# Two encoder layers on one core: the MLP up projection's and the norms' subtractions on VectorE alone, and the second half of the output projection's operands loaded after its first weights

## The chip, the cores and the metric

The kernel runs on one core of a Trainium2 chip. A core has TensorE (PE in the profile, its weight loads PEld), VectorE (DVE), ScalarE (ACT), GpSimd (POOL) and SyncE (SP), whose queue issues the DMAs here. The engines run side by side, each through its own instructions in order, and wait for one another by semaphores. The metric is the device time of one execution in microseconds (us), the median of several runs; lower is better.

## The reference

The trunk has two layers on a sequence of 1024 tokens with 1024 features, in float32. Layer 0 mixes tokens by softmax attention, layer 1 by a gated DeltaNet in both directions; behind each mixer comes a gated MLP with a three-tap convolution:

```python
for i in range(DEPTH):
    y = rmsnorm(h, norm_mix[i])
    h = h + (attention_mixer(y, ...) if i % 2 == 0 else gated_deltanet_mixer(y, ...))
    h = h + conv_ffn(rmsnorm(h, norm_ffn[i]), ...)
return rmsnorm(h, norm_final)

def conv_ffn(h, w_up, conv_w, conv_b, w_down):
    u = depthwise_conv_centred(h @ w_up, conv_w, conv_b)
    a, b = jnp.split(u, 2, axis=-1)
    return (jax.nn.silu(a) * b) @ w_down
```

The DeltaNet ends with `o.reshape(B, S, GDN_V_W) @ w_out`, a projection from 16 heads of 128 to 1024 features.

## The kernel before

**Splits.** A matmul in full precision is made of three in a reduced float32 format. `split` (lines 108 to 110) makes of an operand a rounded part hi (a cast on ScalarE, line 109) and a rest lo = operand - hi (a subtraction on the engine that is passed in, line 110); `dense` (line 134) multiplies hi by hi, hi by lo and lo by hi. Every weight tile and every operand is split so while the kernel runs. In the profile the weights' parts are wh and wl, the tokens' yh and yl, or base (hi) and a lo beside it.

**MLP.** The up projection (`UpProjection`) multiplies 2 x 2 blocks with seven products in place of eight: p1 to p7 with sums and differences of the blocks as operands. `tokens` makes the token side once per layer: the norm's multiplication (line 190), differences of halves (`sub`, line 899), and the splits (`put`) into operands 11, 21, t1, t2, t3, t4 and 22 (t4 and 22 lie in tiles named base). `run` goes over 22 pairs of column tiles f. For each, `operands` loads four weight blocks (a) and makes four sums (s, line 978), `product` splits a sum and issues twelve matmuls into a PSUM bank, and the banks are drained into ua and ub (`first_sum`, line 960, and line 998 on VectorE, copies on ScalarE). Then the convolution (lines 1029 and 1031), the gate's product (line 1035), and `DownProjection.take`, which stores tiles of the result and, in every second f, four differences of them (line 1057) to DRAM. The down projection loads these back as its operands (raw<-g, line 1084). The work of consecutive f overlaps.

In this version GpSimd has a part of those subtractions: in `tokens` every third one, in `operands` the first and third sum, in `product` the splits of p6 and p4, in `take` all four, and in `norm` (line 212) the split of every second tile.

**Output projection of the DeltaNet.** At the end of `gdn` the heads' outputs od lie in DRAM. The first eight heads are multiplied while the last heads are still computed, with partial sums stored as x. For the last eight, `split_rows` loads each od row and splits it, first the first half of the tokens for all eight, then the second half, through three staging tiles t. Then `out_proj` goes over three token ranges (`PARTS`: 512, 256 and 256 tokens) and eight output tiles m: weights (line 121), 24 matmuls, residual from x (line 343), addition (line 344), squares for the next norm. The last partial sums of the first eight heads are added on VectorE (line 818) and stored (line 819) just before.

**Order.** A scheduler sorts all instructions of an engine by priorities, mostly the order of the code; `ahead` raises it. SP issues all loads and stores in one queue in order, so a store that waits for its data holds every load behind it. Tiles of a pool turn round: a load into a staging tile waits until its former content was read.

## Time and profile before

| | |
|---|---|
| median of 3 runs | 3449.74 us (3447.62 to 3450.36) |
| the profiled execution | 3439.26 us, its span 3437.5 us |
| TensorE busy | 3247.3 us, 94% of the span |
| VectorE busy | 2495.2 us, 73% |
| ScalarE busy | 1741.5 us, 51% |
| GpSimd busy | 842.4 us, 25% |

The up projections lie at about 640 to 1090 and 2745 to 3205 us, the DeltaNet from 1310 to 2630, its last output projection from 2644 to 2745. Of a row of the timeline the first number is the start in us from the span's start and the second the duration of the group, with a count behind x where several alike are merged; in brackets stands how long the engine was idle before it, and the instruction that ended that. A matmul's duration is longer than its distance to the next one, since matmuls are pipelined.

### The profile page before, as it was taken

To read this page: it belongs to the slowest core of one execution; us is meant where nothing else is said; L and a number is where in the kernel's file an instruction comes from. 1 tells how busy PE (TensorE), PEld (TensorE's weight loads), DVE (VectorE), ACT (ScalarE), POOL (GpSimd) and SP (SyncE) were. 2 spreads that over 40 slices of the span, in tenths; PEclk is the share of its full clock that TensorE was granted. 3 is DMA by queue.
4 is the path that set the end of the run, shared out by engine and by line. 5 is a ranking of instruction groups with operands and counts; after the bars stand their busy time and mean duration, and the time that the engine had idled before them with its cause. 6 is when DMAs were issued, how large, how long until landed. Compare 5 with 4: busy or idle time off the path is not lost. (4 is left out here: it accounts for less than half of the span.)

```text
span 3437.5 us, 54135 instructions
## 1 busy us (share of the span) xinstructions
PE 3247.3 (94%) x19690; PEld 2620.0 (76%) x19690; DVE 2495.2 (73%) x4235; ACT 1741.5 (51%) x3224; POOL 842.4 (25%) x919
## 2 busy tenths in 40 slices
PE   7999999899999998899999999999898989999998
PEld 6877788677777876677777777777676867777786
DVE  5335886887776875778778787877853787777695
ACT  4235664544454454565555556666532544544453
POOL 1111330444442002121221212222120144444100
PEclk9999999999999999999999999999999999999999
DMA  3331006333324642332342424334356623332743
GB/s 127 104 113 59 32 31 191 122 106 111 112 94 168 218 129 65 102 111 88 113 126 81 136 92 130 102 113 132 102 175 206 204 98 110 101 105 92 244 132 109
DMA packets 249802, 411.20 MB, mean 120 GB/s; under 512 B 25536, under 2 KB 76096, under 8 KB 249536
## 3 DMA queue, kind: packets, MB, share of 16 engines
q1 hardware_dynamic: 249536, 407.76, 36.6%
q8 instruction: 155, 2.54, 0.3%
q14 instruction: 111, 0.91, 0.1%
HBM read 294.80 MB, written 107.61 MB: 117 GB/s over the span
## 5 line engine op out<-in xcount | busy, mean ns | idle before, releaser
L134 PE MATMUL mm<-base,wh 128*128 128x512 f32 x1248 | 480.1, 412 | 10.0 <-ACT base L109 5.9
L109 ACT CAST wh<-w_raw 128x512 fp32r<-128x512 f32 x275 | 169.9, 619 | 296.7 <-PE mm L134 175.6
L110 DVE TENSOR_TENSOR wl<-w_raw,wh 128x512 fp32r<-128x512 f32 x275 | 193.2, 707 | 138.2 <-ACT wh L109 137.1
L134 PE MATMUL mm<-yh,wh 128*128 128x512 f32 x736 | 282.6, 413 | 5.3 <-ACT t L291 2.7
L134 PE MATMUL mm<-yh,wl 128*128 128x512 f32 x736 | 280.6, 410 | 1.0 <-DVE wl L110 1.0
L134 PE MATMUL mm<-yl,wh 128*128 128x512 f32 x736 | 279.3, 408 | 0.3 <-POOL yl L110 0.2
L134 PEld LDWEIGHTS mm<-base,wh 128*128 128x128 f32 x1248 | 238.3, 191 | 49.6 <-ACT base L109 6.3
L153 POOL TENSOR_TENSOR rs<-rs,power 128x8 f32<-128x8 f32 (+2 forms) x38 | 63.8, 1679 | 824.8 <-DVE rs L152 824.7
L134 PE MATMUL mm<-base,wl 128*128 128x512 f32 x624 | 257.3, 412 | 6.4 <-DVE wl L110 6.4
L703 POOL TENSOR_SCALAR kd<-c,yds 128x128 f32<-128x128 f32 x224 | 95.2, 437 | 635.0 <-PE cp L732 444.8
L109 ACT CAST wh<-a 128x512 fp32r<-128x512 f32 x164 | 101.8, 622 | 256.7 <-PE mm L134 122.6
L109 ACT CAST wh<-s 128x512 fp32r<-128x512 f32 x212 | 131.4, 620 | 183.6 <-PE sp L134 87.3
L134 PE MATMUL sp<-base,wh 128*128 128x512 f32 (+1 forms) x672 | 211.5, 372 | 12.6 <-ACT wh L109 12.6
L448 DVE SCALAR_TENSOR_TENSOR t<-mm,gdn_cw,t 128x1023 f32<-128x1023 f32 (+1 forms) x128 | 163.1, 1276 | 6.8 <-ACT t L445 6.1
L134 PEld LDWEIGHTS mm<-yh,wh 128*128 128x128 f32 x736 | 140.6, 193 | 29.3 <-ACT t L291 3.6
L134 PEld LDWEIGHTS mm<-yl,wh 128*128 128x128 f32 x736 | 140.8, 192 | 27.8 <-POOL yl L110 1.6
L134 PEld LDWEIGHTS mm<-yh,wl 128*128 128x128 f32 x736 | 140.8, 191 | 26.5 <-DVE wl L110 1.7
L134 PE MATMUL sp<-base,wl 128*128 128x512 f32 (+1 forms) x432 | 157.7, 365 | 1.4 <-DVE wl L110 0.9
L134 PEld LDWEIGHTS sp<-base,wh 128*128 128x128 f32 x672 | 127.7, 190 | 34.3 <-ACT wh L109 13.0
L110 DVE TENSOR_TENSOR wl<-s,wh 128x512 fp32r<-128x512 f32 x170 | 142.0, 836 | 12.3 <-ACT wh L109 12.2
L978 POOL TENSOR_TENSOR s<-a,a 128x512 f32<-128x512 f32 x80 | 108.5, 1356 | 159.0 <-DVE s L978 106.0
L134 PEld LDWEIGHTS mm<-base,wl 128*128 128x128 f32 x624 | 119.1, 191 | 27.2 <-DVE wl L110 7.2
(522 smaller groups left out, 9362.4 us busy)
## 6 DMA issues: line engine op xcount, KB each, us to landing
a<-in_ffn_up_dram SPq DMA_DIRECT2D x160, 256.0 KB, 2.8
c<-pk SPq DMA_DIRECT2D x128, 320.0 KB, 3.1
w_raw<-in_gdn_in_dram SPq DMA_DIRECT2D x100, 256.0 KB, 2.8
g_t<-t SPq DMA_DIRECT2D x88, 256.0 KB, 2.0
raw<-g_t SPq DMA_DIRECT2D x88, 256.0 KB, 2.6
w_raw<-in_gdn_out_dram SPq DMA_DIRECT2D x68, 256.0 KB, 3.6
g<-t SPq DMA_DIRECT2D x66, 256.0 KB, 2.1
raw<-g SPq DMA_DIRECT2D x66, 256.0 KB, 2.8
```

The costliest lines, as they stand in the source:

```text
L109: self.nc.scalar.copy(out=hi, in_=src)
L110: (engine or self.nc.vector).tensor_tensor(out=lo, in0=src, in1=hi.bitcast(F32), op=ALU.subtract)
L134: self.nc.tensor.matmul(acc if one else acc[:, hs], lhsT=a, rhs=y[:, hs], start=(first and not onto and k + t == 0), stop=(last and k == n ...
L153: nc.gpsimd.tensor_tensor(out=r, in0=v, in1=self.power[:, :w], op=ALU.pow)
L448: nc.vector.scalar_tensor_tensor(out=o, in0=a, scalar=c[:, i:i + 1], in1=o, op0=ALU.mult, op1=ALU.add)
L703: nc.gpsimd.tensor_scalar(out=kd[:, e], in0=kn, scalar1=col(self.yds, e), scalar2=1.0, op0=ALU.mult, op1=ALU.mult)
L978: e.tensor_tensor(out=s[i], in0=x, in1=z, op=op)
```

## The change

Everything that `norm`, `tokens`, `operands`, `product` and `take` gave to GpSimd is given to VectorE. GpSimd keeps the norms' powers (line 153), the softmax's scaling and the DeltaNet's parts. And `split_rows` is cut in two: of the last eight heads only the first half of the tokens is loaded and split before `out_proj`; the second half is loaded by `rest`, called inside `out_proj` after the first four output tiles, through staging tiles od of its own pool ot.

```diff
@@ norm
-                    self.split(y, ys[k][0][:, hs], ys[k][1][:, hs], nc.gpsimd if k % 2 else nc.vector)
+                    self.split(y, ys[k][0][:, hs], ys[k][1][:, hs], nc.vector)
@@ out_proj
-    def out_proj(self, w, ys, res):
+    def out_proj(self, w, ys, res, rest=None):
...
                                 self.squares(self.h[m][:, cs], cs, m)
+                    if rest and cs.start + m0 == 0:
+                        rest(ot)
@@ gdn
-            os = self.split_rows(self.od[8:], oy, HALVES, lambda: tmp.tile([P, S], F32, name="t")[:, :H2])
+            os = self.halved_rows(oy)
+            self.split_into(os, self.od[8:], HALVES[0], lambda: tmp.tile([P, S], F32, name="t")[:, :H2])
             right.close()
...
-            self.out_proj(lambda m: ap["gdn_out"][m][:, 8:], os, lambda m: x[m])
+            self.out_proj(lambda m: ap["gdn_out"][m][:, 8:], os, lambda m: x[m],
+                          lambda ot: self.split_into(os, self.od[8:], HALVES[1], lambda: ot.tile([P, H2], F32, name="od")))
+    def split_into(self, out, rows, hs, stage):
+        for r, pair in zip(rows, out):
+            t = stage()
+            self.nc.sync.dma_start(out=t, in_=r[:, hs])
+            self.split(t, *(x[:, hs] for x in pair))
@@ tokens
         def sub(x, z, out):
-            engine().tensor_tensor(out=out, in0=x, in1=z, op=ALU.subtract)
+            nc.vector.tensor_tensor(out=out, in0=x, in1=z, op=ALU.subtract)
 
         def put(name, k, xs, x):
             hi, lo = self.b[name][k]
-            t.split(x, hi[:, xs], lo[:, xs], engine())
+            t.split(x, hi[:, xs], lo[:, xs])
@@ operands: the four sums, engines gpsimd, vector, gpsimd, vector
-            e.tensor_tensor(out=s[i], in0=x, in1=z, op=op)
+            nc.vector.tensor_tensor(out=s[i], in0=x, in1=z, op=op)
@@ product
-            self.t.split(x, hi, lo, self.nc.gpsimd if name in ("p6", "p4") else self.nc.vector)
+            self.t.split(x, hi, lo)
@@ take
-        sub = lambda out, x, z: nc.gpsimd.tensor_tensor(out=out, in0=x, in1=z, op=ALU.subtract)
+        sub = lambda out, x, z: nc.vector.tensor_tensor(out=out, in0=x, in1=z, op=ALU.subtract)
```

On SP at the start of the DeltaNet's last output projection, the stores of partial sums (x), the loads of the second half (od) and the first weights (w_raw) stood so:

```order
L831 DMA t<-od_22095 128x512
L819 DMA x_27659<-h 128x512
L831 DMA t<-od_22096 128x512
L831 DMA t<-od_24076 128x512
L831 DMA t<-od_24077 128x512
L831 DMA t<-od_26061 128x512
L819 DMA x_27660<-h 128x512
L831 DMA t<-od_26062 128x512
L831 DMA t<-od_27493 128x512
L831 DMA t<-od_27494 128x512
L121 DMA w_raw<-in_gdn_out_dram 128x512 x5
```

Now the same queue has the following rows. The weights stand right behind the last store, eight of them before the first load of the second half; the other six of its loads follow among later weights.

```order
L819 DMA h<-xd_11460 128x512
L821 DMA x_27659<-h 128x512
L821 DMA x_27660<-h 128x512
L121 DMA w_raw<-in_gdn_out_dram 128x512 x5
L343 DMA res<-x_27653 128x512
L121 DMA w_raw<-in_gdn_out_dram 128x512
L343 DMA res<-x_27654 128x512
L121 DMA w_raw<-in_gdn_out_dram 128x512 x2
L843 DMA od<-od_22095 128x512
L843 DMA od<-od_22096 128x512
```

On VectorE in the up projection, the stretch of one odd f from the first convolution step to the draining of the bank of p1 and p2 (ua<-mm, line 960 before and 965 after) stood so:

```order
L1029 SCALAR_TENSOR_TENSOR t_7578<-ua,ffn_cw,t_7578 128x1023
L1031 SCALAR_TENSOR_TENSOR t_7578<-ua,ffn_cw,t_7578 128x1023
L1029 SCALAR_TENSOR_TENSOR t_7582<-ub,ffn_cw,t_7582 128x1023
L1031 SCALAR_TENSOR_TENSOR t_7582<-ub,ffn_cw,t_7582 128x1023
L110 TENSOR_TENSOR wl<-s,wh 128x512
L1035 TENSOR_TENSOR t_7578<-t_7578,t_7582 128x1024
L978 TENSOR_TENSOR s<-a_7601,s 128x512
L960 TENSOR_TENSOR ua<-mm,ua 128x512
```

Now a split (of p6) stands between the first two steps, and in odd f, as here, one difference of `take` (line 1062) ahead of the draining; an even f has the split alone.

```order
L1034 SCALAR_TENSOR_TENSOR t_7578<-ua,ffn_cw,t_7578 128x1023
L110 TENSOR_TENSOR wl<-s,wh 128x512
L1036 SCALAR_TENSOR_TENSOR t_7578<-ua,ffn_cw,t_7578 128x1023
L1034 SCALAR_TENSOR_TENSOR t_7582<-ub,ffn_cw,t_7582 128x1023
L1036 SCALAR_TENSOR_TENSOR t_7582<-ub,ffn_cw,t_7582 128x1023
L110 TENSOR_TENSOR wl<-s,wh 128x512
L1040 TENSOR_TENSOR t_7578<-t_7578,t_7582 128x1024
L983 TENSOR_TENSOR s<-a_7601,s 128x512
L1062 TENSOR_TENSOR t_7590<-t_7578,t_7428 128x512
L965 TENSOR_TENSOR ua<-mm,ua 128x512
```

## Rows read from the trace of the kernel before

**Rows 1.** Windows: us, busy time of PE, PEld, DVE, ACT, POOL (instructions), clock, DMA
```profile
900.00:950.00 50.00, 49.87 (x214) 39.54 (x213) 38.21 (x39) 26.12 (x37) 23.15 (x15) 1.00 0.33 111
2750.00:2800.00 50.00, 41.68 (x153) 30.61 (x154) 38.38 (x61) 21.84 (x45) 24.49 (x22) 0.90 0.27 88
```

**Rows 2.** Timeline of PE where the DeltaNet's last output projection begins
```profile
2631.51 0.39 PE L134 MATMUL mm<-yh,wl 128*128 128x512 f32 x1
2644.47 1.22 PE L134 MATMUL sp<-base,wh 128*128 128x512 f32 x2 [12.57 <-ACT wh L109]
```

**Rows 3.** Timeline of SP's queue in the same stretch
```profile
2636.70 4.10 SPq L831 DMA_DIRECT2D t<-od  x3
2640.85 3.88 SPq L121 DMA_DIRECT2D w_raw<-in_gdn_out_dram  x5
```

**Rows 4.** Timeline of VectorE and ScalarE in the same stretch
```profile
2629.14 1.35 DVE L110 TENSOR_TENSOR base<-t,base 128x512 fp32r<-128x512 f32 x2 [0.62 <-ACT base L109]
2635.39 0.68 DVE L818 TENSOR_TENSOR h<-mm,h 128x512 f32<-128x512 f32 x1
2643.80 0.62 ACT L109 CAST wh<-w_raw 128x512 fp32r<-128x512 f32 x1
```

**Rows 5.** Windows of the same stretch and just behind it
```profile
2640.00:2650.00 10.00, 5.53 (x15) 4.36 (x16) 4.63 (x8) 4.33 (x7) 0.00 (x0) 0.56 0.80 252
2650.00:2660.00 10.00, 10.00 (x45) 8.27 (x45) 2.74 (x4) 1.87 (x3) 0.00 (x0) 1.00 0.54 188
```

**Rows 6.** Line 978: count, duration ns min/median/max, first and last start
```profile
L978 POOL TENSOR_TENSOR s<-a,a x80: 1282/1292/2273, 672.3 to 3176.5; 128x512 f32<-128x512 f32 x80
L978 DVE TENSOR_TENSOR s<-s,a x40: 693/1688/1782, 673.9 to 3174.0; 128x512 f32<-128x512 f32 x40
L978 DVE TENSOR_TENSOR s<-a,s x40: 678/684/692, 694.0 to 3189.1; 128x512 f32<-128x512 f32 x40
```

**Rows 7.** Timeline of PE, DVE and POOL in one f, and the last f's p5
```profile
901.62 1.74 POOL L110 TENSOR_TENSOR wl<-a,wh 128x512 fp32r<-128x512 f32 x1
903.41 0.50 PE L134 MATMUL sp<-base,wl 128*128 128x512 f32 x1
913.56 0.68 DVE L960 TENSOR_TENSOR ua<-mm,ua 128x512 f32<-128x512 f32 x1
914.00 0.40 PE L134 MATMUL sp<-t23h,wl 128*128 128x512 f32 x1
914.39 0.47 PE L134 MATMUL mm<-t10h,wh 128*128 128x512 f32 x1
...
3190.50 0.47 PE L134 MATMUL mm<-t10h,wh 128*128 128x512 f32 x1
```

**Rows 8.** Timeline of POOL, DVE and PE where both up projections begin
```profile
636.32 0.69 POOL L153 TENSOR_TENSOR rs<-rs,power 128x2 f32<-128x2 f32 x1
656.25 1.43 DVE L110 TENSOR_TENSOR base<-h,base 128x256 fp32r<-128x256 f32 x4
658.49 4.68 DVE L110 TENSOR_TENSOR base<-h,base 128x256 fp32r<-128x256 f32 x4
663.83 0.50 PE L134 MATMUL mm<-base,wl 128*128 128x512 f32 x1 [3.46 <-DVE wl L110]
...
2779.50 0.80 PE L134 MATMUL mm<-base,wl 128*128 128x512 f32 x1 [2.94 <-DVE wl L110]
2812.57 0.71 PE L134 MATMUL mm<-t10h,wh 128*128 128x512 f32 x1 [2.73 <-DVE ua L960]
```

**Rows 9.** Timeline of SP's queue, POOL and PE where both down projections begin
```profile
1093.53 4.53 SPq L1056 DMA_DIRECT2D g_t<-t  x3
1096.42 1.29 POOL L1057 TENSOR_TENSOR t<-t,t 128x512 f32<-128x512 f32 x1 [1.22 <-DMA g<-t]
1105.86 0.67 PE L134 MATMUL mm<-gh,base 128*128 128x512 f32 x1 [2.70 <-ACT base L109]
...
3222.75 0.50 PE L134 MATMUL mm<-gh,base 128*128 128x512 f32 x1 [1.97 <-ACT base L109]
```

More of the change, by code (lines that the diff above doesn't have):

```diff
@@ L808, in gdn @@
                 self.head_out(j, o, dp)
-            os = self.split_rows(self.od[:8], oy, [slice(0, S)], lambda: tmp.tile([P, S], F32, name="t"))
+            os = self.split_rows(self.od[:8], oy, lambda: tmp.tile([P, S], F32, name="t"))
             x = [self.dram.tile([P, S], F32, name=f"x{m}") for m in range(KT)]
@@ L823, in gdn, with split_rows @@
             self.psum = self.banks(sp=4)
-            self.out_proj(lambda m: ap["gdn_out"][m][:, 8:], os, lambda m: x[m])
-    def split_rows(self, rows, pool, parts, stage):
+            self.out_proj(lambda m: ap["gdn_out"][m][:, 8:], os, lambda m: x[m],
+                          lambda ot: self.split_into(os, self.od[8:], HALVES[1], lambda: ot.tile([P, H2], F32, name="od")))
+    def split_rows(self, rows, pool, stage):
         out = self.halved_rows(pool)
-        for ps in parts:
-            for r, pair in zip(rows, out):
-                t = stage()
-                self.nc.sync.dma_start(out=t, in_=r[:, ps])
-                for hs in HALVES if len(parts) == 1 else [ps]:
-                    self.split(t[:, hs] if len(parts) == 1 else t, *(x[:, hs] for x in pair))
-        return out
+        for r, pair in zip(rows, out):
+            t = stage()
+            self.nc.sync.dma_start(out=t, in_=r)
+            for hs in HALVES:
+                self.split(t[:, hs], *(x[:, hs] for x in pair))
+        return out
+    def split_into(self, out, rows, hs, stage):
+        for r, pair in zip(rows, out):
+            t = stage()
+            self.nc.sync.dma_start(out=t, in_=r[:, hs])
+            self.split(t, *(x[:, hs] for x in pair))
     def halved_rows(self, pool):
@@ L891, in tokens @@
         t, nc, h = self.t, self.nc, self.t.h
-        n = [0]
-        def engine():
-            n[0] += 1
-            return nc.vector if n[0] % 3 else nc.gpsimd
         def sub(x, z, out):
-            engine().tensor_tensor(out=out, in0=x, in1=z, op=ALU.subtract)
+            nc.vector.tensor_tensor(out=out, in0=x, in1=z, op=ALU.subtract)
         def put(name, k, xs, x):
             hi, lo = self.b[name][k]
-            t.split(x, hi[:, xs], lo[:, xs], engine())
+            t.split(x, hi[:, xs], lo[:, xs])
         with t.ahead(1):
@@ L975, in operands @@
         s = [slot("s") for _ in range(4)]
-        for i, (x, z, op, e) in enumerate(((a21, a22, ALU.add, nc.gpsimd), (s[0], a11, ALU.subtract, nc.vector),
-                                           (a11, a21, ALU.subtract, nc.gpsimd), (a12, s[1], ALU.subtract, nc.vector))):
-            e.tensor_tensor(out=s[i], in0=x, in1=z, op=op)
+        for i, (x, z, op) in enumerate(((a21, a22, ALU.add), (s[0], a11, ALU.subtract), (a11, a21, ALU.subtract),
+                                        (a12, s[1], ALU.subtract))):
+            nc.vector.tensor_tensor(out=s[i], in0=x, in1=z, op=op)
         return {"p1": (a11, "11"), "p2": (a12, "21"), "p5": (s[0], "t1"), "p6": (s[1], "t2"), "p7": (s[2], "t3"),
```

## The prediction

> **What bounds the kernel now.** I read the windows of 50 us first. In the middle of an up projection TensorE is busy for 49.87 of 50 us, with 214 matmuls, 0.233 us each; VectorE has 38.21 and GpSimd 23.15 [rows 1]. There TensorE is the bound, and work that moves between the other two engines can win back only what is left of waits. Where an up projection begins the picture is another one: 41.68 of 50 us and only 153 matmuls [rows 1]. So I then read the timeline of TensorE for its idle times, and what ended each. Three places are touched by the change. At the start of the DeltaNet's last output projection TensorE is idle for 12.57 us until ScalarE has cast the first weights [rows 2]. At the start of both up projections it waits 3.46, 2.94 and 2.73 us, each time for VectorE [rows 8]. At the start of both down projections it waits 2.70 and 1.97 us for a cast of an operand that came late from DRAM [rows 9].
>
> **VectorE and GpSimd together.** The sums of line 978 show what a subtraction of 128 x 512 costs. GpSimd takes 1.29 us for it, VectorE 0.684 us alone; the same form at the place where it runs beside GpSimd's has a median of 1.688 us [rows 6]. So 1.00 us of that row is a price of company, and it is VectorE that pays it. The 128 x 256 splits tell the same: four in 1.43 us, 0.36 each, and the next four, of the same line and tiles, in 4.68 us [rows 8]. A moved 512-wide operation therefore adds at most 0.68 us to VectorE and gives back between 0 and 1.00 us, by how much of GpSimd's 1.29 us met a VectorE operation.
>
> **Part 1, the output projection's second half.** TensorE ends the last product of the first eight heads at 2631.51 + 0.39 = 2631.90. Its sum is added on VectorE only at 2635.39, behind splits of the second half; then its store goes out, three loads of the second half hold SP from 2636.70 to 2640.80 because they wait for staging tiles, and the first weights go out at 2640.85 [rows 3, 4]. From that issue it is 2.95 us to the cast at 2643.80 [rows 3, 4] and 3.62 us to the first matmul at 2644.47 [rows 2]. Now the splits of the first half, which end at 2629.14 + 1.35 = 2630.49 [rows 4], are the last thing on VectorE before that addition. So: 2631.90 + 0.1 + 0.68 for the addition, 0.63 for the store (as from 2636.07, where the addition ends now, to the next issue at 2636.70), weights issued at about 2633.3 and the first matmul at 2633.3 + 3.6 = 2636.9. That is 7.6 us earlier.
>
> What the moved step brings with it: eight loads, eight casts, eight subtractions, now beside the matmuls of the first token range, 192 of them or 192 x 0.233 = 44.7 us. VectorE is busy for 2.74 and ScalarE for 1.87 of 10 us there [rows 5], and the eight pairs need 8 x (0.62 + 0.68) = 10.4 us in all, so they fit. But they stand in queues: the second-half loads have two staging tiles, so each pair waits for the pair before it, SP holds the weights behind it, and ScalarE holds the casts of weights behind the casts of od. One round is 2.95 + 0.62 + 0.68 = 4.3 us; a weight tile feeds 12 matmuls, 2.8 us. If each of the three later pairs held TensorE for a round less one tile, that would be 3 x 1.5 = 4.5 us; ahead of the first pair stand eight weight tiles, 22 us of work, and three tiles can be cast in advance, so I take 1 us. The clock: the stretch 2640 to 2650 was granted 0.56 on average, so part of it ran at 1.2 GHz, behind the idle time, and 2650 to 2660 was at 1.00 again [rows 5]; the first two matmuls span 1.22 us. An idle time of 5 us may lead to the same or not; if not, up to 2.2 us more are won (half of the 4.4 us from 2644.47 to about 2649). I take no difference. Term: 7.6 - 1 = **6.6 us**, bounds 3.1 (7.6 - 4.5) and 9.8 (7.6 + 2.2).
>
> **Part 2, the steady up projection.** In the f shown, p5's first matmul starts at 914.39, 0.39 us behind the one before it in place of 0.233 [rows 7]. It starts 0.15 us after the draining of the bank on VectorE ends (913.56 + 0.68 = 914.24), and so it stands up to the last f of the second layer, whose p5 starts at 3190.50 [rows 7]: VectorE's queue up to this draining decides in the 19 steady f of either layer. Together with the next matmul this costs some 0.2 us per f. In every second f p4 waits for GpSimd's split as well (901.62 + 1.74 = 903.36, the matmul at 903.41 [rows 7]), another 0.2 us. So at most 19 x (0.2 + 0.1) = 5.7 us per layer, 11 in both, can be won.
>
> The change puts 2 sums, 2 splits and on average 2 differences per f on VectorE, 6 x 0.68 = 4.1 us of the 19.8 us that an f takes; its 38.21 of 50 us are 15.1 us per f [rows 1], which would be 19.2, of which the company of GpSimd goes off again. Of the six only those ahead of the draining matter: the order shows the p6 split in every f and one difference in odd f. Without relief the draining comes 0.68 us later in even and 1.36 in odd f. With the relief of 1.00 us [rows 6] for one operation in front of it, it comes 0.3 earlier and 0.4 later, and p4's wait is gone. I take the latter: even f win 0.2, odd f lose 0.25, p4 wins 0.2 in every second one, 0.15 us per pair, 10 pairs in either layer: **3 us**, bounds +11 us won and, without relief, 38 x 1.0 = 39 us lost.
>
> **Part 3, the beginnings of the up projections.** 26 of the 80 operations of `tokens` per layer move to VectorE, most 256 wide: 26 x 0.4 = 10 us more of its time. It is at its limit there: p3's rest part (wl) stands behind the splits into base before and after the change. But these splits cost 4.68 in place of 1.43 us beside GpSimd [rows 8], 3.2 us in one row of four, and the power for the second norm (636.32) stood on GpSimd behind splits [rows 8], which are gone from its queue. The waits at stake are 3.46 + 2.94 + 2.73 = 9.1 us, and about 2 for that power. I take half: **5 us**; bounds 11 won and 4.5 lost, the latter if of the 10 us per layer 3.2 come back and TensorE waits for a third of the rest.
>
> **Part 4, the beginnings of the down projections.** SP is held from 1093.53 to 1098.06 by three stores of differences that wait for GpSimd, whose last ends at 1096.42 + 1.29 = 1097.71 [rows 9]; the loads that TensorE waits for at 1105.86 stand behind them. On VectorE each takes 0.61 us less, but they stand among the splits of weights, and the last still waits for a store's landing. I take 1 us per layer, **2 us**; bounds 0 and 4.7 (2.70 + 1.97).
>
> **Part 5, the norms.** 16 splits, 8 in each mixer's norm, move, each 0.61 us shorter on VectorE (1.29 - 0.68 [rows 6]). But VectorE also does the multiplications in front of them and has 8 x 0.68 = 5.4 us more to do, so what a split wins the next multiplication waits for: **0**, bounds 1 either way.
>
> **The sum.** 6.6 + 3 + 5 + 2 = 16.6 us. The profiled execution took 3439.3, so it would take 3422.7. The median of the runs shown is 3449.7, 10.5 longer; the same difference gives **3433**.
>
> **A rule against the change.** VectorE's time beside GpSimd is longer by the rows above. The Trainium skill (Perfetto Trace Analysis, Optimizing Scalar/DVE Operations) says that with a saturated DVE it may pay to hand work even to GPSIMD, and warns in the same breath that the two share an SBUF read port, so that it might not help. By its first half taking the work back costs time, as in the second rival below; by its warning it is a gain, and rows 6 speak for the warning.
>
> **Rivals.** *Only the output projection gains.* VectorE in one queue has to do what two engines did, and each wait for GpSimd comes back as a wait for VectorE: parts 2, 3 and 4 sum to nothing. For it: VectorE's gaps in steady work are small, and 15.1 of 19.8 us per f was with GpSimd's help. Against it: rows 6. The time is 3449.7 - 6.6 = 3443. Chance 0.25.
>
> *VectorE becomes the bound of the up projection (slower).* The draining of p1's and p2's bank is late by the moved operations in front of it, without relief. It decides from the point where it ends more than 0.2 us later than now behind the same matmul, since p5 already starts 0.15 us behind it. Price 39 us at the most; with parts 1 and 4 to its credit (8.6) it gives 3449.7 + 39 - 8.6 = 3480, and at half the price 3461. For it: in the steady f nothing lies between the draining and TensorE. Against it: the relief. Chance 0.08.
>
> *Everything closes.* All waits named go, with the clock's 2.2: 9.8 + 11 + 11 + 4.7 = 36.5 at the most, some 28 in the middle, 3422. Chance 0.12.
>
> *The second half comes too late.* The order moves the loads as the change says, so that it does nothing is excluded; but weights held in SP's and ScalarE's queues could take back 4.5 us or more, and the projection only gains 2: 3438 with the other parts. Chance 0.05. The forecast, 3428 to 3440, has 0.50.
>
> **The numbers.** The range leaves out the slower rival and the lower third of the one in which everything closes: 3421 to 3446. About 0.2%, 6.9 us, is what a measurement of this kernel can tell from no change. Below 3442.8 lie the forecast almost whole (0.49), half of the first rival (0.12), the third (0.12) and most of the fourth (0.04): faster 0.77. Same 0.15, slower 0.08.
>
> **What would show it.** The idle time before the output projection's first matmul is about 5 us, its weights are issued right behind the last store, and no wait over 1 us for a cast of weights follows. Line 983 on VectorE has one duration, about 0.69 us. The first matmul of p5 starts on time in even f and 0.2 to 0.4 us late in odd f; an f takes 19.7 to 19.8 us on average. The waits for wl at the beginnings are shorter, not gone. I am wrong if f takes over 20.2 us, if the casts of od hold weights, or if the beginnings of the up projections grow by what VectorE takes over.

## The result: some 33 us less, twice the forecast

| | before | after |
|---|---|---|
| median on the first chip | 3450.05 us (3447.62 to 3450.39) | 3415.91 us (3414.59 to 3417.39) |
| profiled execution, its span | 3439.26, 3437.5 us | 3417.39, 3415.4 us |
| GpSimd busy | 842.4 us | 369.1 us |
| VectorE busy | 2495.2 us | 2534.8 us |

The ratio is 0.990, 95% interval 0.989 to 0.992: 34.1 us faster. On two other chips it was 29.9 us (0.991, 0.990 to 0.993) and 36.4 us (0.990, 0.988 to 0.991). The forecast was 3433, 16.6 us faster, with a range from 3421 to 3446; the time lies below it. The sign was right. The size was not: the gain is twice the 16.6 us.

GpSimd lost 473 us of work, and VectorE gained only 40 us. The windows of after in which [rows 1] were read (columns as there: PE, PEld, DVE, ACT, POOL with their instructions, clock, DMA) show how:

```profile
900.00:950.00 50.00, 49.80 (x217) 40.22 (x216) 39.47 (x55) 23.20 (x35) 0.00 (x0) 1.00 0.36 116
2750.00:2800.00 50.00, 42.71 (x164) 32.77 (x165) 46.26 (x85) 26.78 (x48) 0.00 (x0) 0.90 0.30 97
```

In the steady stretch VectorE executes 55 operations in place of 39 and is busy for 39.47 us in place of 38.21. A longer stretch says it better, the 18 steady f of the first layer in before and in after:

```profile
716.35:1072.88 356.53, 355.39 (x1514) 281.75 (x1512) 274.82 (x275) 176.32 (x257) 161.22 (x108) 1.00 0.29 100
705.00:1058.31 353.31, 351.54 (x1514) 283.24 (x1513) 290.88 (x383) 177.18 (x257) 0.00 (x0) 1.00 0.31 101
```

VectorE has 108 operations more. Those that follow one another start 0.60 us apart (rows of part 2 below), so 64.8 us would be added; 16.1 were. So some 49 of the 274.8 us that VectorE had been busy, about a sixth, were the price of GpSimd's company. Added up by operation, what each takes beyond the shortest of its form, it is 48.5 us in before and 2.7 in after. Line 983 (978 before) in the trace of after, with durations as minimum, median and maximum in ns, has one price for all forms, where [rows 6] had medians of 684 and 1688 on VectorE and 1292 on GpSimd:

```profile
L983 DVE TENSOR_TENSOR s<-a,a x80: 679/683/692, 663.4 to 3152.2; 128x512 f32<-128x512 f32 x80
L983 DVE TENSOR_TENSOR s<-s,a x40: 679/689/694, 664.1 to 3151.0; 128x512 f32<-128x512 f32 x40
L983 DVE TENSOR_TENSOR s<-a,s x40: 681/685/689, 683.0 to 3165.9; 128x512 f32<-128x512 f32 x40
```

**Where the time went.** The next table cuts the execution at the starts of certain matmuls, in three traces of before and three of after (the pairs above and the repetitions below). "Beginning" is the stretch up to the first matmul of p5 in the fourth f, from attention's last product with v in the first layer, and in the second from the 171st matmul of the output projection.

| stretch | before, us | after, us | difference of means | forecast |
|---|---|---|---|---|
| start to the first product with v | 290.9 to 292.1 | 285.3 to 286.8 | -5.4 | 0 (part 5) |
| beginning of the first up projection | 187.6 to 188.7 | 181.7 to 181.8 | -6.6 | -5 for both (part 3) |
| 18 steady f, first layer | 356.5 to 356.6 | 353.3 | -3.2 | -1.5 (part 2) |
| down projection, first layer | 201.1 to 203.8 | 198.1 to 202.0 | -2.1 | -1 (part 4) |
| norm and projections before the DeltaNet | 130.6 to 133.1 | 131.8 to 133.7 | +0.5 | 0 (part 5) |
| DeltaNet | 1164.7 to 1168.8 | 1165.9 to 1173.0 | +3.7 | none |
| wait before the last output projection | 12.6 to 13.0 | 6.0 to 6.5 | -6.6 | -6.6 (part 1) |
| its first 171 matmuls | 40.3 to 41.5 | 40.1 to 40.5 | -0.5 | in part 1 |
| beginning of the second up projection | 145.3 to 148.7 | 139.2 to 141.9 | -7.3 | with the first |
| 18 steady f, second layer | 356.6 | 353.3 | -3.3 | -1.5 |
| down projection, second layer | 198.5 to 199.5 | 196.6 to 199.6 | -0.5 | -1 |

The stretches whose ranges lie apart give 5.4 + 6.6 + 3.2 + 6.6 + 7.3 + 3.3 = 32.4 us. The other rows have ranges that overlap, and stretches that the table leaves out differ by less than 1 us in the mean.

### The profile page after: what moved, and what is told of

It is laid out like the page before. It is cut to its first block, busy times and chain, and to the rows that moved or that the text cites. A ratio compares the mean times of both kernels' runs of the same rounds, so it can differ in the third digit from the quotient of the medians.

```text
span 3415.4 us, 53938 instructions
## 1 busy us (share of the span) xinstructions
PE 3233.7 (95%) x19690; PEld 2618.6 (77%) x19690; DVE 2534.8 (74%) x4567; ACT 1749.4 (51%) x3226; POOL 369.1 (11%) x587
## 5 line engine op out<-in xcount | busy, mean ns | idle before, releaser
L134 PEld LDWEIGHTS mm<-yl,wh 128*128 128x128 f32 x736 | 140.2, 191 | 26.3 <-DVE yl L110 1.3
L134 PEld LDWEIGHTS mm<-yh,wl 128*128 128x128 f32 x736 | 140.1, 190 | 24.9 <-DVE wl L110 0.6
L109 ACT CAST gh<-raw 128x512 fp32r<-128x512 f32 x132 | 81.7, 619 | 114.7 <-DMA raw<-g_t 60.4
L110 DVE TENSOR_TENSOR wl<-a,wh 128x512 fp32r<-128x512 f32 x164 | 112.6, 686 | 34.4 <-ACT wh L109 31.0
```

The source lines that it names most:

```text
L109: self.nc.scalar.copy(out=hi, in_=src)
L110: (engine or self.nc.vector).tensor_tensor(out=lo, in0=src, in1=hi.bitcast(F32), op=ALU.subtract)
L134: self.nc.tensor.matmul(acc if one else acc[:, hs], lhsT=a, rhs=y[:, hs], start=(first and not onto and k + t == 0), stop=(last and k == n ...
```

## What the executions of one kernel differ by

> The kernel before, once more, for a second profile. The profiled execution of before took 3439.3 us, 10.5 less than the median of its timed runs, and the one of after 3417.4, 1.5 more than its own; so the two traces differ by 22.1 us and the medians by 34.1. Theory A: the DeltaNet between 1400 and 2625 us of the first trace of before ran faster than it usually does; a second trace has it 8 to 10 us longer, all other stages within 1 us, and a span near 3448. Rival B: the change makes the DeltaNet slower (in the two traces it takes 9 us longer after the change), and the other stages of before differ from run to run; then the DeltaNet of this trace takes the same 1225 us within 1 us as in the first one, and the span differs elsewhere.

It took 3441.9 us, and its DeltaNet 1166.4 us, 1.7 more than in the first trace: theory A falls as stated. Rival B missed its own 1 us, but it seemed to hold, since eleven traces without all of before's GpSimd work, taken up to then, had 1167 to 1174 us there. So it was tested once more, later:

> The kernel before a third time, for the DeltaNet alone: 1163.6 to 1166.4 us in three traces that have before's GpSimd work, 1167.2 to 1173.5 in eleven that do not, with the same order of instructions from 60 us on. Theory: the change makes it longer: 1163 to 1167 again. Rival: it is chance, since the granted clock in it differs from trace to trace: 1168 or more.

1168.8 us, 3445.9 in all: the rival, by its number. norm_h1 below, with the changed kernel's DeltaNet, took 1164.5, and only_up below, with before's, 1172.1. So this stretch takes 1164 to 1174 us, and which kernel runs doesn't settle where in between. That it is chance alone is not shown: the four traces that keep all that GpSimd had average 1165.9 us, the sixteen others 1170.0. A loss of some 4 us there by the change stays open; the timed medians, 33.5 us of gain on average over the three chips where the stretches above sum to 32.4, speak against it.

From 60 us after its start on, the order of instructions on every engine is the same in the traces compared. What goes with the time is the clock: in the eleven traces below 1169 us the granted clock is 0.50 for 41 to 51 us of this stretch, in the nine from 1171 up for 51 to 61. One place shows it. The same matmuls in the repetition of after (after_again) and in that of before (before_again; windows, columns as above):

```profile
1985.00:1990.00 5.00, 5.00 (x44) 3.73 (x43) 2.81 (x7) 2.56 (x7) 0.00 (x0) 0.50 0.07 27
1990.00:1995.00 5.00, 5.00 (x39) 3.95 (x39) 2.77 (x6) 1.96 (x5) 1.37 (x3) 0.67 0.00 0
```
```profile
2005.00:2010.00 5.00, 5.00 (x60) 4.01 (x57) 4.81 (x14) 4.36 (x10) 0.00 (x0) 1.00 0.23 69
```

In the first the granted clock is 0.50 (1.2 GHz) with 44 matmuls in 5 us, and this place costs 4.5 us against the second, where it is 1.00 (2.4 GHz) with 60. Just before, TensorE had waited 1.60 us in the first and 1.06 in the second.

On the second chip single executions of before took 3436.0 to 3449.5. Between the first two traces lie 22.1 us, the medians are 34.1 apart, and 8.3 of the difference is the DeltaNet alone (1164.7 and 1173.0). My step "the median is 10.5 longer; the same difference gives 3433" moves the forecast from that one execution to the median and leaves the gain at 16.6 us, so it isn't what made the forecast wrong.

## The two halves

The output projection's change alone (before, with `rest`, `split_into` and the call of `out_proj` as in the diff above), the rest alone, and both:

> Before, with the output projection's part of the change alone (second half of its operands loaded behind its first weights); GpSimd keeps all that it had. Theory: the two halves of the change add up. In the traces the first matmul of the projection comes 7.2 us earlier against its surroundings, so 7 us of the 34 come from here: 3443, ratio 0.998. Rival: this part also moves the loads of the second up projection's beginning, and part of the gain there (7 us in the traces) hangs on it: 10 to 14 us, 3436 to 3440.

3439.1 us against 3442.9, ratio 0.9985 (0.9975 to 0.9995): 3.8 us by the medians, 1.7 to 8.6 by the interval. The times expected were counted from the first chip's 3450, so it is the gain that decides: the theory's 7 lies in the interval, the rival's 10 to 14 do not. In its trace the wait is 6.1 us, not 13, and the beginning of the second up projection takes 145.5, as before. The rival falls.

> After, with the output projection's operands loaded as before; everything that was taken from GpSimd stays on VectorE. Theory: 34 - 7 = 27 us faster than before, 3423, ratio 0.992; the output projection's idle time is 12 to 13 us again. Rival: the halves do not add up, and this one gives 20 us or less.

3417.1 us, 25.7 less (0.993, 0.991 to 0.994), with a wait of 12.5 us. 3.8 + 25.7 = 29.5.

> The changed kernel, timed on this chip with the others and for a second profile. Theory: 34 us faster than before, 0.990; stages of the trace within 1 us of the first trace, the DeltaNet apart, which varies by some us from run to run. Rival: what varies lies in the stages that the change touches.

3413.0 us, 29.9 less. The halves add up. The stages did not all keep to 1 us of the first trace of after: the down projections take 198.1 and 196.6 in place of 202.0 and 198.9, the second beginning 139.2 in place of 141.9. So a scatter of 2 to 4 us lies in stages that the change touches as well.

## Part 1, the output projection

The first matmul was forecast some 5 us behind the last one of the first eight heads, with weights issued right behind the last store. The timelines of PE, VectorE and SP in after, which answer [rows 2 to 4]:

```profile
2631.90 1.22 PE L134 MATMUL sp<-base,wh 128*128 128x512 f32 x2 [5.59 <-ACT wh L109]
```
```profile
2626.34 0.69 DVE L820 TENSOR_TENSOR h<-mm,h 128x512 f32<-128x512 f32 x1 [1.76 <-PE mm L134]
```
```profile
2622.32 5.06 SPq L821 DMA_DIRECT2D x<-h  x2
2627.43 2.34 SPq L121 DMA_DIRECT2D w_raw<-in_gdn_out_dram  x5
```

The addition comes 0.04 us behind the last matmul's end (2625.91 + 0.39), the weights go out 0.4 us behind the addition's end, and the first matmul 4.47 us behind that. Forecast were 0.1, 0.63 and 3.6. The wait is 5.59 us in place of 12.57, so 7.0 are gone, and nothing of them comes back: no other matmul of this projection waits over 1 us for its weights, and its first 171 matmuls take 40.3 us on average, 40.9 before. The queue's 1 us was not paid; 0.9 us went into the weights' way instead. That the term came out at 6.6 is in part luck: two misses of about 1 us cancel.

## Parts 2 and 4: the up projection and its differences

Each GpSimd part was given back to it alone, in the changed kernel (e is GpSimd for the first and third sum, VectorE for the others).

```diff
@@ operands (keep_up)
-            nc.vector.tensor_tensor(out=s[i], in0=x, in1=z, op=op)
+            e.tensor_tensor(out=s[i], in0=x, in1=z, op=op)
@@ product (keep_up)
-            self.t.split(x, hi, lo)
+            self.t.split(x, hi, lo, self.nc.gpsimd if name in ("p6", "p4") else self.nc.vector)
@@ take (keep_take)
-        sub = lambda out, x, z: nc.vector.tensor_tensor(out=out, in0=x, in1=z, op=ALU.subtract)
+        sub = lambda out, x, z: nc.gpsimd.tensor_tensor(out=out, in0=x, in1=z, op=ALU.subtract)
```

> After, but the first and third sum of the weight blocks and the splits of p6 and p4 are on GpSimd again. Theory: the steady f are back at 356.5 us for 18 in place of 353.3, in both layers; the beginnings keep most of their gain (within 2 us of after). Rival: the differences of the last tiles also hold GpSimd or VectorE, and the steady f come to between 354 and 356; or the beginnings lose 5 us or more, as the other run's rival has it.

> After, but the four differences of result tiles that the down projection needs (in every second f) are on GpSimd again. In after an even f takes 19.49 us and an odd one 19.77 to 19.79, in before 19.77 and 19.85. Theory: the odd f differ since VectorE has this difference ahead of the draining; without it odd f take 19.5 as well and 18 steady f 351 us. Rival: the company of GpSimd costs VectorE as much as the difference did, and 18 f take 353 to 356. The start of the down projections (from the last f's p5 to the last product, 196.6 to 202 us in after) is not told apart by either.

And the first of the two parts alone in before (only_up):

> Before, with one part of the change alone: the first and third sum and the splits of p6 and p4 on VectorE; the differences for the down projection, the tokens and the norms keep GpSimd, and the output projection loads as before. Theory: this part alone has the steady gain, 349.6 us for 18 f in either layer (7 less than before), and the beginnings' gain, 6 us from the attention's end to the fourth f (187.7 in before, 181.7 in after); the DeltaNet, whose instructions are the same, takes 1163 to 1167 us as in the three traces with before's GpSimd work. Rival: the steady gain needs the other parts as well (353 or more); the DeltaNet takes 1168 or more as in the eleven traces of after and its relatives.

| kernel | beginning, layer 0 | 18 f | beginning, layer 1 | 18 f |
|---|---|---|---|---|
| before (mean of three) | 188.3 | 356.5 | 147.4 | 356.6 |
| after (mean of three) | 181.7 | 353.3 | 140.1 | 353.3 |
| keep_up | 187.9 | 361.3 | 148.2 | 361.4 |
| keep_take | 182.1 | 349.6 | 140.7 | 349.5 |
| only_up | 185.3 | 349.5 | 140.2 | 349.5 |
| keep_tokens (below) | 181.5 | 353.3 | 138.8 | 353.6 |

In this part the change is two changes that pull against each other. The sums and the splits of p6 and p4 win 7.0 us per layer (356.5 to 349.5). The differences of `take` on VectorE lose 4.8 without the other part (356.5 to 361.3) and 3.7 with it (349.6 to 353.3). Both theories had another value: keep_up was to be at 356.5 and came to 361.3, keep_take at 351 and came to 349.6. only_up has the theory's 349.6 in both layers (349.5). VectorE's timeline up to the draining (L960, then L965) tells why, in an even f of before and of after and an odd one of keep_take:

```profile
865.51 1.28 DVE L1029 SCALAR_TENSOR_TENSOR t<-ua,ffn_cw,t 128x1023 f32<-128x1023 f32 x1 [0.76 <-ACT t L1028]
868.64 1.72 DVE L1029 SCALAR_TENSOR_TENSOR t<-ub,ffn_cw,t 128x1023 f32<-128x1023 f32 x1 [0.52 <-ACT t L1028]
...
873.33 0.68 DVE L978 TENSOR_TENSOR s<-a,s 128x512 f32<-128x512 f32 x1
873.93 0.68 DVE L960 TENSOR_TENSOR ua<-mm,ua 128x512 f32<-128x512 f32 x1
874.53 1.45 DVE L110 TENSOR_TENSOR wl<-s,wh 128x512 fp32r<-128x512 f32 x1
```
```profile
853.07 1.28 DVE L1034 SCALAR_TENSOR_TENSOR t<-ua,ffn_cw,t 128x1023 f32<-128x1023 f32 x1 [0.71 <-ACT t L1033]
854.27 0.69 DVE L110 TENSOR_TENSOR wl<-s,wh 128x512 fp32r<-128x512 f32 x1
...
860.32 0.69 DVE L983 TENSOR_TENSOR s<-a,s 128x512 f32<-128x512 f32 x1
860.92 0.68 DVE L965 TENSOR_TENSOR ua<-mm,ua 128x512 f32<-128x512 f32 x1
861.52 0.68 DVE L110 TENSOR_TENSOR wl<-s,wh 128x512 fp32r<-128x512 f32 x1
```
```profile
871.34 1.28 DVE L1034 SCALAR_TENSOR_TENSOR t<-ua,ffn_cw,t 128x1023 f32<-128x1023 f32 x1 [0.71 <-ACT t L1033]
...
879.19 0.69 DVE L965 TENSOR_TENSOR ua<-mm,ua 128x512 f32<-128x512 f32 x1
879.79 1.19 DVE L110 TENSOR_TENSOR wl<-s,wh 128x512 fp32r<-128x512 f32 x1
880.91 1.78 DVE L983 TENSOR_TENSOR s<-a,a 128x512 f32<-128x512 f32 x1
```

None of the three has a difference on VectorE ahead of the draining. From the first convolution step's start to the draining's it is 8.42 us in before and 7.85 in after and keep_take, although one split more stands between them. In an odd f after has one difference of `take` (L1062) more there, 0.60 us from start to start, and is at 8.46 us, where before was at 8.38. So p5 starts on time in every second f of after only: two f in a row take 39.26 us (19.49 and 19.77), where before took 39.63 (19.77 and 19.86). keep_take takes 38.83, and no p5 waits. There TensorE is the bound, with 219 matmuls in the window in which [rows 1] has 214:

```profile
900.00:950.00 50.00, 50.00 (x219) 40.67 (x218) 39.17 (x48) 24.26 (x36) 11.10 (x5) 1.00 0.35 110
```

Part 2 of the prediction had this shape and the wrong sizes. "Even f win 0.2, odd f lose 0.25, p4 wins 0.2 in every second one" is 0.15 us per two f; it was 0.37. Two things were off. Operations that follow one another start 0.60 us apart, and not the 0.68 of their duration that I had added up. And the relief was not the 1.00 us of one operation but whatever GpSimd had touched in that stretch: 1.1 us, nearly enough to pay for both new operations of an odd f. My slower rival is what keep_up shows: there the difference stands ahead of the draining and GpSimd still lengthens a convolution step. Its timelines of VectorE and PE, in two neighbouring f:

```profile
864.85 2.29 DVE L1036 SCALAR_TENSOR_TENSOR t<-ua,ffn_cw,t 128x1023 f32<-128x1023 f32 x1
```
```profile
852.98 0.47 PE L134 MATMUL mm<-t10h,wh 128*128 128x512 f32 x1 [0.73 <-DVE ua L965]
```

Its profile took 3445.4 us, where the run of before beside it had 3440.2.

GpSimd is a good place for `take` because the operations that it lengthens there lie behind the draining (1.19 and 1.78 us in keep_take's rows above), where TensorE has work before it needs them. GpSimd's own durations grow too: of one form of line 1062 in keep_take the shortest took 1364 ns and the median 3068:

```profile
L1062 POOL TENSOR_TENSOR t<-t x22: 1364/3068/3173, 676.1 to 3161.0; 128x512 f32<-128x512 f32 x22
```

**Part 4.** The down projection was forecast 1 us shorter per layer, because its differences' stores hold SP. In after the last of these stores no longer hold SP for 4.53 us [rows 9], but the first wait is still there (SP, then PE):

```profile
1078.67 1.95 SPq L1061 DMA_DIRECT2D g_t<-t  x2
...
1082.88 0.32 SPq L1061 DMA_DIRECT2D g_t<-t  x1
```
```profile
1091.39 0.50 PE L134 MATMUL mm<-gh,base 128*128 128x512 f32 x1 [2.92 <-ACT base L109]
```

2.92 us, 2.70 before [rows 9]. In both layers of all twenty traces it lies between 1.2 and 3.1 us, with the differences on either engine. The 2 us can't be told from chance; the step that a store's delay sets this wait is not borne out.

## Part 3: the beginnings

In the changed kernel every third operation of `tokens` was put back on GpSimd (`engine()` as in before):

> After, but in the up projection's preparation of the tokens every third operation is given to GpSimd again. From the attention's last product to the first p5 the traces before took 117.0 us and those after 110.0; in the second layer from 40 us into the output projection to the fourth f's p5, 146 to 149 before and 139 to 142 after. Theory: the beginnings' gain comes from here: these stretches are back at 116 to 117 and at 146 or more, the steady f as after (353.3 us for 18). Rival: it comes from the sums and the splits of p6 and p4 of the first f, which lie in the same stretch; then they stay at 110 to 111 and 140 to 142.

The first p5 came 6.0 us later, as the theory has it, and the fourth f at the same time (181.5 against 181.7 us; in the second layer 138.8 against 140.1). So what `tokens` wins up to the first p5 is given back by the fourth f, and in the changed kernel this part is worth nothing. The rival holds, from the table above: with the sums and splits on GpSimd the beginnings are at 187.9 and 148.2, as in before, and keep_up's own theory that they keep their gain falls. only_up shows that these alone win the whole gain in the second layer (140.2) and 3 of 6.6 us in the first (185.3); the other half is there once either `tokens` or `take` leaves GpSimd as well (182.1, 181.5). Where they cost is seen on PE, in keep_up and then in after:

```profile
649.34 0.79 PE L134 MATMUL sp<-t30h,wh 128*128 128x512 f32 x1 [5.47 <-ACT t30h L109]
659.91 0.51 PE L134 MATMUL sp<-t20h,wh 128*128 128x512 f32 x1 [2.39 <-ACT wh L109]
...
692.32 0.50 PE L134 MATMUL sp<-t30h,wh 128*128 128x512 f32 x1 [2.32 <-ACT ua L1021]
```
```profile
648.12 0.79 PE L134 MATMUL sp<-t30h,wh 128*128 128x512 f32 x1 [5.18 <-ACT t30h L109]
657.79 0.51 PE L134 MATMUL sp<-t20h,wh 128*128 128x512 f32 x1 [0.47 <-ACT wh L109]
685.44 0.50 PE L134 MATMUL sp<-t30h,wh 128*128 128x512 f32 x1 [0.97 <-ACT ua L1021]
```

The cast wh that p6 waits for at 659.91 needs the second sum, and that one needs the first, which takes 2.30 us on GpSimd in keep_up and 0.68 on VectorE in after:

```profile
655.02 2.30 POOL L983 TENSOR_TENSOR s<-gh,gl 128x512 f32<-128x512 f32 x1 [8.81 <-DVE h L904]
```
```profile
655.12 0.68 DVE L983 TENSOR_TENSOR s<-gh,gl 128x512 f32<-128x512 f32 x1
```

The trace of before had it already. What GpSimd did beside the four splits that took 4.68 us [rows 8] is a split of a weight and two sums of `operands`, not work of `tokens`; GpSimd's timeline in before:

```profile
658.24 1.47 POOL L110 TENSOR_TENSOR wl<-gl,wh 128x512 fp32r<-128x512 f32 x1
659.67 1.49 POOL L978 TENSOR_TENSOR s<-gh,gl 128x512 f32<-128x512 f32 x1
661.10 1.46 POOL L978 TENSOR_TENSOR s<-gh 128x512 f32<-128x512 f32 x1
```

Part 3 of the prediction took the three waits that name VectorE and the one for the power, and "half" of them. In after none of the three is left, nor the one for the power in the first layer; waits of 5.18 and 4.89 us at the first p7 of the two layers came in, where before had 1.05 and 1.66. The term left out all waits that name a cast on ScalarE, though the cast is late because of what was subtracted ahead of it; and it put the cause into `tokens`. Both beginnings won 14 us, beyond its bound of 11.

**A try that moved a wait.** The 5.18 us at the first p7 are VectorE's own: it makes t4 and 22 of the first quarter before t3 of the second.

```diff
         for xs, y in ys:
             for k in range(4):
                 sub(y[k + 4][1], y[k][1], y[k][1])
                 put("t3", k, xs, y[k][1])
+        for xs, y in ys:
             for k in range(4):
```

> keep_take_5, and in the preparation of the tokens the operands t3 are made for both quarters before t4 and 22. In after TensorE waits 5.18 and 4.89 us in the first f for the second quarter of t3 (first matmul of p7), while VectorE makes t4 and 22 of the first quarter. Theory: p7 starts 2 to 4 us earlier, and the fourth f of either layer too, with 4 to 8 us in both; 28 to 34 us, in all 42 to 45 us faster than before. Rival: VectorE has the same sum of work up to the end of the preparation, so that p4 and p3, which need t4 and 22, wait instead: the fourth f is where it was, within 1 us.

3412.4 us (0.991, 0.990 to 0.993), 8 slower by the median than keep_take_5 beside it, with intervals that overlap a little. PE in its trace:

```profile
645.34 0.49 PE L134 MATMUL sp<-t30h,wh 128*128 128x512 f32 x1 [1.57 <-ACT t30h L109]
654.81 1.22 PE L134 MATMUL mm<-base,wh 128*128 128x512 f32 x2 [6.19 <-ACT ub L1024]
```

The wait for t3 fell to 1.57 us and a wait of 6.19 came behind it. The fourth f is 1.7 us later than in keep_take in the first layer and 4.1 in the second: worse than the rival's nothing.

> t3_first, with every third operation of the preparation on GpSimd as in keep_tokens. There the first p5 came 6.0 us later than in after and the fourth f at the same time, so that this part of the change gave nothing. Theory: once the order lets TensorE start p7 early, the preparation is bound by VectorE's work, and here the engine that helps is worth what its company costs: fourth f within 1 us of t3_first. Rival: with help it is 2 us or more earlier (67 operations less on VectorE), or later.

179.8 and 141.0 us up to the fourth f, 3.9 and 3.8 less than t3_first: the rival (its 67 operations are 52 by the traces). With that order help is worth its company, presumably because VectorE has too much to do at once. Against keep_take it is 2.2 us better in one layer and 0.3 worse in the other; 3407.3 in its one run.

## Part 5: the first norm

keep_norm has this edit in the changed kernel; norm_h0 and norm_h1 have the condition `k % 2 and i == 0` or `i == 1`, and norm_y4 has bufs=4 for y beside it:

```diff
-                    self.split(y, ys[k][0][:, hs], ys[k][1][:, hs], nc.vector)
+                    self.split(y, ys[k][0][:, hs], ys[k][1][:, hs], nc.gpsimd if k % 2 else nc.vector)
```

> After, but the norms in front of the mixers give every second split to GpSimd again. From the start to the first product of the attention's weights with v (first ph) the traces before took 290.9 to 291.1 us and those after 285.2 to 285.8. Theory: the norm at the start is the cause, since its multiplication writes into a tile y with two buffers and so waited for GpSimd to have read one (1.36, 0.66, 0.69 us and so on, 3.8 us in all in the trace of before): this stretch is back at 290 to 291 us, all other stages as after. The prediction held this part for 0: then the stretch stays at 285.5.

291.7 us to the first product with v, as in before (290.9 to 292.1), the other stages as after: the forecast's 0 is refuted. All traces agree: the six with every second split on GpSimd and two tiles y have 290.8 to 292.1 us, the eleven with all of them on VectorE 283.5 to 286.8. The timeline of VectorE in before, then those of VectorE and PE in keep_norm:

```profile
24.29 0.75 DVE L190 SCALAR_TENSOR_TENSOR y<-base,norm_mix,mm 128x512 f32<-128x512 f32 x1 [1.36 <-POOL yl L110]
```
```profile
25.03 0.75 DVE L190 SCALAR_TENSOR_TENSOR y<-base,norm_mix,mm 128x512 f32<-128x512 f32 x1 [1.36 <-POOL yl L110]
27.82 0.75 DVE L190 SCALAR_TENSOR_TENSOR y<-base,norm_mix,mm 128x512 f32<-128x512 f32 x1 [0.66 <-POOL yl L110]
```
```profile
27.00 0.80 PE L134 MATMUL mm<-yh,wh 128*128 128x512 f32 x1 [1.12 <-ACT wh L109]
29.23 0.79 PE L134 MATMUL mm<-yh,wl 128*128 128x512 f32 x1 [1.00 <-DVE wl L110]
```

The multiplication waits until GpSimd has read one of two tiles y, and the first rest of weights waits behind it. Is that the cause of the 6 us?

> keep_norm (every second split of the norms on GpSimd), but with four buffers of y in place of two. keep_norm took 291.7 us from the start to the first product with v, 6.2 more than after. Theory: VectorE's multiplications stood still because GpSimd had not yet read the tile; with four buffers they do not, and 4 us or more of the 6 come back: 285.5 to 288. Rival: it is GpSimd's 1.29 us in front of TensorE, or its company, that costs; then it stays at 290 or more.

294.3: it took longer still, on the rival's side. VectorE waits for no tile there, but its order became another one, and TensorE waited 4.54 us for the first wl. So this run doesn't tell; the edit took the wait away and put VectorE's work in front of TensorE's.

> After, with every second split of the norms on GpSimd again for the first half of the tokens alone. keep_norm lost 6.2 us up to the first product with v; with four buffers of y it lost no less, but there the order of VectorE was another one too (a rest of weights 4.5 us late). Theory: the loss is made where TensorE begins: its first rest of weights stands behind a multiplication that waits for GpSimd, and TensorE stays at the lower clock longer; then this kernel shows 4 us or more of the 6 (289.5 or more). Rival: it is made in the second half; then 287 or less.

> The same for the second half of the tokens alone. Theory: it shows at most 2 us of the 6 (287.5 or less to the first product with v). Rival: 4 us or more (289.5).

287.5 and 287.0: the theory on the first half falls. Each half alone costs 1 to 1.5 us over the 286.0 of after, hardly more than the scatter of traces with all splits on VectorE; both together cost 5.7. The traces show where. Up to the 48th matmul of the projections behind the norm keep_norm is 4.1 us behind after and norm_h0 3.3; at the 192nd norm_h0 has 1.7 left and keep_norm has 5.8. In between TensorE waits twice for a power on GpSimd in keep_norm and in before (1.32 and 1.78 us), and once in after and with either half. What is shown is that the splits of this norm on GpSimd cost it; by which path, and why the halves don't add up, stays open. The same splits in front of the DeltaNet cost nothing that the traces tell (134.3 us, 131.8 to 133.7 in after).

## A version that leaves `take` on GpSimd

keep_take has all of the change but the differences of `take`.

> The same kernel as keep_take (after, with the four differences for the down projection on GpSimd), timed. In its first trace 18 steady f took 349.6 us in either layer, against 353.3 in after and 356.5 in before. Theory: the two layers give 7.4 us and nothing takes them back, so it is 6 to 8 us faster than after, 36 to 38 faster than before on one chip (ratio 0.989). Rival: the DeltaNet or the down projections take them back, and it is as fast as after.

3404.1 us, 37.0 less than before (0.989, 0.987 to 0.991). Side by side with the changed kernel:

> The changed kernel, timed beside the next one on the same chip. Over all profiles an execution of it takes 3406.5 to 3415.4, by the DeltaNet's chance of some 10 us. Theory: 28 to 34 us faster than before.

> After, with the four differences for the down projection on GpSimd. Theory: 18 steady f take 3.7 us less in either layer and nothing gives them back, so it is 5 to 9 us faster than the changed kernel on the same chip. Rival: within 3 us of it, because the beginnings (0.4 and 1.5 us longer in one trace) and the norm after the layer take part of it back.

3408.3 and 3403.8: 4.5 us by the medians, between theory and rival, and the intervals are almost the same (0.9899 with 0.988 to 0.991, and 0.9894 with 0.988 to 0.991). By three traces of either kernel the steady f win 3.7 + 3.8 us. That part is shown. The beginnings are 0.4 and 1.2 us longer in the mean, the down projections 1.9 and 1.8, the norm and projections before the DeltaNet 1.8, all but the first with ranges that overlap; together that is almost as much as the steady f win. So that this kernel is faster as a whole is not shown.

## Why the forecast was wrong, point by point

The direction and the mechanism, relief from GpSimd's company, were right. Three terms of the sum were too small: the beginnings (5 forecast, 14 measured), the norms (0 and 5.4) and the steady up projection (3 and 6.5). These are 18 us too little, about the 17.5 by which the forecast's gain is short.

- **The output projection** (6.6): 6.6 us of wait are gone. "No difference in clock" (0.50 for 3.8 us behind the first matmul in the first trace of after, 4.4 in that of before) and "no wait over 1 us" held; within the sum, the weights' way 0.9 longer and the queue's 1 us not paid cancel.
- **The steady up projection** (3): shape right, size 6.5. The term counted durations where starts count, and a single operation's relief. An f takes 19.63 us, below the 19.7 to 19.8 forecast.
- **The beginnings** (5): 14. "I take half" was wrong, as was "shorter, not gone": the named waits are all gone. The waits that name ScalarE belonged to the term, and the cause was in `operands` and `product`, not in `tokens`.
- **The down projections** (2): nothing that can be told.
- **The norms** (0): 5.4 at the start. "What a split wins the next multiplication waits for" took VectorE for the one that is waited for; in before its multiplication waits for GpSimd (the 1.36 us above). Whether that wait makes the 5.4 is not shown.
- **The company of GpSimd.** Rows 6 named the price, 1.00 us of 1.688, and I let it count for one operation in front of the draining. It is about a sixth of VectorE's busy time (some 49 of 274.8 us in 18 f). The Trainium skill (Perfetto Trace Analysis, Optimizing Scalar/DVE Operations) warns that GPSIMD and DVE share an SBUF read port, so that moving work between the two might not help. The traces agree in that VectorE's operations lengthen, by that number; that a port is the reason they don't show. The same section of the Trainium skill says that handing work even to GPSIMD may make sense if DVE is saturated. VectorE is not saturated here (39.17 of 50 us in keep_take), and still GpSimd is the better place for `take` in the steady f: 3.7 us per layer.
- **The rivals.** "Everything closes" (0.12; 3422, at most 36.5 us gained) was nearest to the size, by other sums than its own: it had 11 for the beginnings and nothing for the norm. Since all parts rested on the same relief, its chance should have been larger. The 39 us of the slower one's bound are 38 by its own factors; nothing hangs on it.

## What to carry to other kernels

Before costing a move between VectorE and GpSimd, compare the same operation alone and in company, and apply the difference to all that VectorE does beside GpSimd, not to the moved operation. What falls behind the last operation that TensorE waits for can stay on GpSimd; in the steady f here it was the better place. In a full queue count from start to start; and where a wait names a cast, look for what the cast waited for.

## What the runs showed of the hardware

- Beside GpSimd VectorE's subtraction of two 128 x 512 tiles takes up to 1.8 us in place of 0.68, and a convolution step 2.29 in place of 1.28. GpSimd pays as well: 3.07 us in the median for a subtraction whose shortest took 1.36 (line 1062 in keep_take).
- Operations on VectorE that follow one another start sooner than their durations say: 0.60 us apart at 0.68.
- Executions of one kernel on one chip differ by up to 20 us (only_vec, 3408.8 to 3428.9). The DeltaNet makes 7 between two traces of the changed kernel; the granted clock there was 0.50 for some us in one execution and 1.00 at the same matmuls in another.
